# A Conformer block on one core: its depthwise convolution on TensorE in four token phases and plain float32, with more taps on ScalarE and Pool

## The chip, the cores and the metric

The kernel runs on one core of one Trainium2 chip. The metric is the device time of one execution in microseconds (us). The median of three runs before the change is 1697.9 us (1696.76 to 1698.34).

## What is computed

The program is a two-part model on 512 tokens of 1024 channels in float32. The part that the change touches is the first thing that runs, the convolution module:

```
def conformer_conv(h, w_pw1, b_pw1, w_dw, b_dw, ln_g, ln_b, w_pw2, b_pw2):
    u = h @ w_pw1 + b_pw1
    a, gate = jnp.split(u, 2, axis=-1)
    u = a * jax.nn.sigmoid(gate)
    u = lax.conv_general_dilated(
        u, w_dw[:, None, :], window_strides=(1,), padding=[(CONV_WIDTH - 1, 0)],
        dimension_numbers=("NWC", "WIO", "NWC"), feature_group_count=CONV_CHANNELS) + b_dw
    u = jax.nn.silu(layernorm(u, ln_g, ln_b))
    return u @ w_pw2 + b_pw2
```

`h` is the RMS-normed input and `CONV_WIDTH` is 31: each channel is convolved with its own 31 taps over the tokens. After it come a SwiGLU layer, dilated attention, another SwiGLU layer, a retention and pooling mixer and a gated feed-forward layer. They are about nine tenths of the time and the change leaves them alone.

## The kernel before

Channels lie on the 128 partitions and the 512 tokens along them, so the 1024 channels are eight tiles, j = 0 to 7. A large matrix product is made in three passes: each operand is split into a rounded high part and the rest (`whi`, `wlo` of the weights; `xh`, `xl` of the activations), and `mm3` multiplies high by high, high by rest and rest by high. `Stream` brings weights: SP loads a chunk into one of four `raw` buffers, ScalarE writes `whi`, and VectorE (for some chunks Pool) writes `wlo` and so frees the buffer.

In the conv stage the order on TensorE is the list `SEQ`. `g3` is the group of matmuls of tile 3 (an `a` half and a gate half, 48 matmuls into two PSUM banks of a ring of six). `conv_start` then calls `gated`: VectorE multiplies the gate half by the row norm (`tg`), ScalarE takes the sigmoid, VectorE multiplies the `a` half (`ta`, into SBUF), and a last VectorE instruction adds the bias, multiplies the two and writes `up`. The banks of the group come free when VectorE has read them.

From `up` the tiles go two ways:

- Tiles 0, 2, 4 and 5 (`JV`): 31 multiply-adds over shifted views of `up` (`conv_tile`), in two chains `ca` and `cb` in PSUM on VectorE. `POOLT[j]` of the taps are made by ScalarE (the product `tp`) and Pool (the sum `cp`) and added to the rest in `end`. `keep_up` decides by estimated costs how many of these instructions are put in after each half-tick of matmuls.
- Tiles 1, 3, 6 (`JP`) and 7 (`JS`): `to_phases` reorders `up` by SP DMAs so that the partition holds 2 token phases x 64 channels. TensorE multiplies by 128x128 matrices that Pool builds from the taps (`matrices`, buffers `dg`), again in high and low parts (`c1a` and `c1b` in `SEQ` are the two channel groups of tile 1). ScalarE copies the result out of PSUM, SP DMAs reorder it back into `cx`, and one VectorE instruction (`back`) adds the bias and the mean shift `nm0` and writes `cc`.

All DMAs stand in one queue, SP's, in program order, and a DMA that waits holds up all behind it. In it are also six DMAs (`bias_vectors`, `bd` and `be`) that write a table for the later attention through DRAM and read it back. VectorE, ScalarE and Pool each run strictly in program order too. `shift_of_first` makes `nm0` from tile 0 by one matmul (`m`). The layer norm then takes its sums from the squares (`ssq`) and the sum of all tiles (`lnb`, by Pool); its first matmul on all tiles is `lne`.

Of the kernel before, what the change touches and what calls it, by code (L numbers as in the profile page):

```python
# [50 lines left out]
PARTS = 2  # L51
# [6 lines left out]
class Meter:  # L58
# [144 lines left out]
def phases(w):  # L203

    r = np.zeros((2, 64, len(JP) + 1, 2, CW + 1), w.dtype)
    for n, j in enumerate(JP + (JS,)):
        t = w[:, 128 * j:128 * j + 128].reshape(CW, 2, 64).transpose(2, 1, 0)
        r[0, :, n, :, 1:] = t
        r[1, :, n, :, :CW] = t
# [60 lines left out]
def body(nc, tc, A, out):  # L270
# [3 lines left out]
    with ctx:  # L274
# [275 lines left out]
        with tc.tile_pool(name="c1", bufs=1) as c1, tc.tile_pool(name="c1s", bufs=1, side="right") as c1s:  # L550
# [3 lines left out]
            def utile(name, shape=(128, PAD + S), dt=F32):  # L554
                return c1.tile(list(shape), dt, tag="u", name=name, bufs=NU)
# [3 lines left out]
            ct = [c1s.tile([128, S + (PAD if j in JP + (JS,) else 0)], F32, name=f"cc{j}") for j in range(KD)]  # L559
# [41 lines left out]
            def high_part(t):  # L601

                h = utile("hp", t.shape, F32R)
                ACT.activation(out=h, in_=t, func=AF.Copy)
                return h.bitcast(F32)

            V.tensor_tensor(out=wpl, in0=wp, in1=high_part(wp), op=ALU.subtract)

            def matrices(key, n, w, wl, idt):

                d = []
                for src in (w, wl):
                    t = c1.tile([128, 2048], F32R, tag="dg", name="dg", bufs=6)
                    d.append(t)
                    m = idt.shape[1]
                    for a in range(0, n, n // 2 if n % 2 == 0 else n):
                        b = min(n, a + (n // 2 if n % 2 == 0 else n))

                        def build(t=t, src=src, a=a, b=b):
                            G.tensor_tensor(  # L620
                                out=t[:, m * a:m * b].rearrange("p (a b) -> p a b", b=m),
                                in0=idt.unsqueeze(1).to_broadcast([128, b - a, m]),
                                in1=src[:, a:b].unsqueeze(2).to_broadcast([128, b - a, m]),
                                op=ALU.mult,
                            )

                        mat_q.append((key, build))
                dgs[key] = d
# [110 lines left out]
            def gated(j, pa, pg, dst):  # L739
                tg = tmp.tile([128, S], F32, tag="t1", name="tg")  # L740
                V.tensor_tensor(out=tg, in0=pg, in1=R, op=ALU.mult)
                ACT.activation(out=tg, in_=tg, func=AF.Sigmoid, bias=col("b_pw1", 8 + j))
                ta = tmp.tile([128, S], F32, tag="t2", name="ta")
                V.tensor_tensor(out=ta, in0=pa, in1=R, op=ALU.mult)
                run_q(dve_q, 1)
                cut = (lambda v: v) if len(dst.shape) == 2 else (lambda v: v.rearrange("c (s p) -> c p s", p=2))
                V.scalar_tensor_tensor(out=dst, in0=cut(ta), scalar=col("b_pw1", j), in1=cut(tg), op0=ALU.add, op1=ALU.mult)
# [17 lines left out]
            def to_phases(j, a):  # L765

                t = ct[j]
                tv = t.rearrange("p (g s) -> p g s", g=2)
                av = a.rearrange("c (p s) -> c p s", p=2)
                for g in range(2):  # L770
                    for p in range(2):
                        nc.sync.dma_start(out=tv[64 * p:64 * p + 64, g], in_=av[64 * g:64 * g + 64, p])

                def parts():
                    if j == JS:
                        ACT.activation(out=tj[:, :, 0], in_=tv, func=AF.Copy)
                        V.tensor_tensor(out=tj[:, :, 1], in0=tv, in1=tj[:, :, 0].bitcast(F32), op=ALU.subtract)
                        return
                    h, l = utile("uth", dt=F32R), utile("utl", dt=F32R)
                    ACT.activation(out=h, in_=t, func=AF.Copy)  # L780
                    V.tensor_tensor(out=l, in0=t, in1=h.bitcast(F32), op=ALU.subtract)
                    ud[j] = [x.rearrange("p (g s) -> p g s", g=2) for x in (h, l)]

                after(PARTS, parts)

            def conv_phases(j, g):
                if g == 0:
                    bc[j] = xbank("oj")
                o = bc[j].rearrange("p (g s) -> p g s", g=2)[:, g]
                dh, dl = built((j, g))  # L790
                h, l = ud[j]
                for d in range(HP + 1):
                    c = slice(128 * d, 128 * d + 128)
                    mm3(o, dh[:, c], dl[:, c], h[:, g, d:d + HS], l[:, g, d:d + HS], d == 0, d == HP)
                if g == 1:
                    y, x = cc[j], utile("cx", (128, S))
                    ACT.copy(y, bc[j])
                    yv = y.rearrange("p (g s) -> p g s", g=2)
                    xv = x.rearrange("c (q s) -> c q s", q=2)
                    for g in range(2):  # L800
# [29 lines left out]
            units = [(int(x[1]), "ab".index(x[2])) for x in SEQ.split() if x[0] == "c"]  # L830
# [17 lines left out]
            for x in SEQ.split():  # L848
# [16 lines left out]
            def conv_half(h, n0=0, n1=64):  # L865
                ov = o7[h].rearrange("p (g l s) -> p g l s", g=2, l=2)
                for n in range(n0, min(n1, 2 * (HP + 1))):
                    g, d = n // (HP + 1), n % (HP + 1)
                    c = slice(128 * d, 128 * d + 128)
                    s_ = slice(128 * h + d, 128 * h + d + 128)  # L870
                    PE.matmul(ov[:, g], djs[g][0][:, c], tj[:, g, :, s_], start=(d == 0), stop=False)
                    PE.matmul(ov[:, g, 0], djs[g][1][:, c], tj[:, g, 0, s_], start=False, stop=(d == HP))

            def half_out(h):
                ov = o7[h].rearrange("p (g l s) -> p g l s", g=2, l=2)
                y = tmp.tile([128, S], F32, tag="t1", name="y7")
                z = y[:, 256:512].rearrange("p (g s) -> p g s", g=2)
                y = y[:, 0:256].rearrange("p (g s) -> p g s", g=2)
                ACT.copy(z, ov[:, :, 1])
                V.tensor_tensor(out=y, in0=ov[:, :, 0], in1=z, op=ALU.add)  # L880
                y7[h] = y
# [25 lines left out]
            zs = [c1.tile([128, 4, S], F32R, tag="dg", name="zs", bufs=6) for _ in range(4)]  # L907
# [733 lines left out]
```

## Time and profile before

| | before |
|---|---|
| profiled execution | 1698.02 us, its span 1696.2 us |
| TensorE busy | 1655.6 us, 98% of the span |
| VectorE busy | 884.8 us, 52% |
| ScalarE busy | 577.7 us, 34% |
| Pool busy | 187.3 us, 11% |
| granted TensorE clock | 0.989 of full |

Busy time says how long an engine had something in it; it does not say what ended last. The conv stage lies in the first 185 us of the span, and there the shares are others: in the first 180 us TensorE is busy for 160.7 us, VectorE for 149.6 us and Pool for 119.0 us.

### The profile page before, as it was taken

To read this page: it belongs to the slowest core of one execution; us is meant where nothing else is said; L and a number is where in the kernel's file an instruction comes from. 1 tells how busy PE (TensorE), PEld (TensorE's weight loads), DVE (VectorE), ACT (ScalarE), POOL (GpSimd) and SP (SyncE) were. 2 spreads that over 40 slices of the span, in tenths; PEclk is the share of its full clock that TensorE was granted. 3 is DMA by queue.
4 is the path that set the end of the run, shared out by engine and by line. 5 is a ranking of instruction groups with operands and counts; after the bars stand their busy time and mean duration, and the time that the engine had idled before them with its cause. 6 is when DMAs were issued, how large, how long until landed. Compare 5 with 4: busy or idle time off the path is not lost.

```text
span 1696.2 us, 20102 instructions
## 1 busy us (share of the span) xinstructions
PE 1655.6 (98%) x8044; PEld 1391.1 (82%) x8044; DVE 884.8 (52%) x1277; ACT 577.7 (34%) x858; POOL 187.3 (11%) x152
## 2 busy tenths in 40 slices
PE   8988999999999999999999999999999999999997
PEld 6877888888888888888888888888888888888886
DVE  7898654444443445654444443346775545444226
ACT  4133532323322334343323323234543534333210
POOL 4778200000000000000000000000322200000000
PEclk9989999999999999999999999999999999999999
DMA  6322133333232342123333322332232233333321
GB/s 185 113 75 64 39 112 100 99 100 98 86 102 94 93 120 80 51 87 100 100 100 99 100 89 92 106 117 82 63 102 61 83 105 100 100 100 100 99 87 50
DMA packets 154822, 158.11 MB, mean 93 GB/s; under 512 B 6393, under 2 KB 147304, under 8 KB 154728
## 3 DMA queue, kind: packets, MB, share of 16 engines
q1 hardware_dynamic: 154728, 156.83, 30.3%
q8 instruction: 63, 1.03, 0.3%
q14 instruction: 31, 0.25, 0.1%
HBM read 152.79 MB, written 3.95 MB: 92 GB/s over the span
## 4 chain that ended last, share of the span: by engine, by line
PE 81%; DVE 11%; ACT 3%; issue 2%; SPq 1%; DMA 1%; POOL 1%; DVEq 0%; ACTq 0%; POOLq 0%
PE mm L73 69%; PE dn L73 6%; DVE cb L73 2%; PE pv L73 2%; DVE wlo L73 2%; DVE ca L73 2%; PE o L73 1%; PE po L73 1%; DVE cc L73 1%; DVE y L73 1%; ACT whi L120 1%; PE s L73 1%; DVE P L73 1%; DVE up L73 1%; DVE rp L73 0%
## 5 line engine op out<-in xcount | busy, mean ns | idle before, releaser
L73 DVE TENSOR_TENSOR wlo<-raw,whi 128x1024 fp32r<-128x1024 f32 (+1 forms) x278 | 336.0, 1222 | 520.7 <-ACT whi L120 520.1
L73 PE MATMUL mm<-xh,whi 128*128 128x512 f32 (+1 forms) x1472 | 572.4, 389 | 1.8 <-ACT xh L580 1.7
L73 PE MATMUL mm<-xl,whi 128*128 128x512 f32 (+1 forms) x1472 | 568.8, 386 | 2.4 <-POOL xl L73 1.9
L73 PE MATMUL mm<-xh,wlo 128*128 128x512 f32 (+1 forms) x1472 | 568.9, 386 | 1.9 <-DVE wlo L73 1.9
L120 ACT ACTIVATE whi<-raw 128x1024 fp32r<-128x1024 f32 (+1 forms) x282 | 285.8, 1031 | 520.6 <-PE mm L73 324.8
L73 PEld LDWEIGHTS mm<-xl,whi 128*128 128x128 f32 x1472 | 278.4, 189 | 59.4 <-DVE xl L73 3.1
L73 PEld LDWEIGHTS mm<-xh,whi 128*128 128x128 f32 x1472 | 278.7, 189 | 58.4 <-ACT xh L580 2.1
L73 PEld LDWEIGHTS mm<-xh,wlo 128*128 128x128 f32 x1472 | 278.2, 189 | 57.9 <-DVE wlo L73 2.5
L73 PE MATMUL mm<-hh,whi 128*128 128x512 f32 x352 | 136.9, 389 | 0.0
L73 PE MATMUL mm<-hl,whi 128*128 128x512 f32 x352 | 136.9, 389 | 0.0
L73 PE MATMUL mm<-hh,wlo 128*128 128x512 f32 x352 | 136.9, 389 | 0.0
L73 POOL TENSOR_TENSOR r<-v,mhalf 128x4 f32<-128x4 f32 x9 | 13.8, 1531 | 993.2 <-DVE v L73 993.2
L73 PEld LDWEIGHTS mm<-hh,wlo 128*128 128x128 f32 x352 | 66.1, 188 | 13.8
L73 PEld LDWEIGHTS mm<-hl,whi 128*128 128x128 f32 x352 | 66.1, 188 | 13.7
L73 PEld LDWEIGHTS mm<-hh,whi 128*128 128x128 f32 x352 | 66.1, 188 | 13.6
L73 PE MATMUL dn<-whi,gh 128*128 128x512 f32 x176 | 68.7, 390 | 0.9 <-DVE a L73 0.9
L73 PE MATMUL dn<-wlo,gh 128*128 128x512 f32 x176 | 68.6, 390 | 0.1
L73 PE MATMUL dn<-whi,gl 128*128 128x512 f32 x176 | 68.5, 389 | 0.0
L970 ACT ACTIVATE hh<-b 128x512 fp32r<-128x512 f32 x44 | 27.8, 632 | 79.5 <-DVE b L73 79.5
L73 DVE TENSOR_TENSOR b<-mm,R 128x512 f32<-128x512 f32 x44 | 30.2, 685 | 44.5 <-PE mm L73 44.5
L966 ACT ACTIVATE a<-a 128x512 f32<-128x512 f32 x44 | 27.8, 632 | 72.6 <-DVE a L73 72.6
L73 DVE TENSOR_TENSOR hl<-b,hh 128x512 fp32r<-128x512 f32 x44 | 30.5, 692 | 30.8 <-ACT hh L970 30.8
(265 smaller groups left out, 1881.6 us busy)
## 6 DMA issues: line engine op xcount, KB each, us to landing
raw<-in_ffn_w_gate SPq DMA_DIRECT2D x44, 512.0 KB, 4.2
raw<-in_ffn_w_up SPq DMA_DIRECT2D x44, 512.0 KB, 3.8
raw<-in_w_up SPq DMA_DIRECT2D x44, 512.0 KB, 4.0
raw<-in_ffn_w_down SPq DMA_DIRECT2D x40, 512.0 KB, 3.5
raw<-in_w_down SPq DMA_DIRECT2D x22, 512.0 KB, 3.3
raw<-in_w_in SPq DMA_DIRECT2D x20, 512.0 KB, 3.6
raw<-in_attn_w_qkv SPq DMA_DIRECT2D x18, 512.0 KB, 3.8
raw<-in_conv_w_pw SPq DMA_DIRECT2D x30, 256.0 KB, 6.3
```

What stands on the lines that cost most here:

```text
L73: return fn(*args, **kw)
L120: self.nc.scalar.activation(out=hv, in_=raw, func=AF.Copy)
L966: ACT.activation(out=a, in_=a, func=AF.Silu)
L970: ACT.activation(out=hh[j], in_=b, func=AF.Copy)
```

## The change

Tiles 1, 3 and 6 go through TensorE in four token phases x 32 channels instead of two x 64, and in plain float32 with one matmul where there were three with split operands. The matrices of a tile are four groups of nine, 128x128, and are multiplied with 128 tokens each. Tile 7 stays in two phases, but also in plain float32. So the splits of the phase data (`uth`, `utl`, `tj`) and of the taps (`wpl`) go. The reordering of tiles 1, 3 and 6 takes 16 DMAs of 32 partitions each way instead of 4 of 64. The taps on ScalarE and Pool of tiles 0, 2, 4, 5 go from 4, 0, 3, 6 to 7, 8, 8, 8. `gated` writes the product of the `a` half back into its PSUM bank and reads it from there. `SEQ` names the four groups, and the cost estimate counts a plain float32 matmul four times. The line of the helper that records VectorE, Pool and TensorE instructions moves from L73 to L79.

```diff
-SEQ = "g0 g1 g2 g3 c1a c1b g4 g5 c3a g6 c3b g7 c6a c6b"
-POOLT = {0: 4, 1: 2, 3: 4, 5: 6, 4: 3, 2: 0}
+SEQ = "g0 g1 g2 g3 c1ab c1cd g4 g5 c3ab g6 c3cd g7 c6ab c6cd"
+POOLT = {0: 7, 2: 8, 4: 8, 5: 8}
+NPH = 4
+PPAD = 32
+NB = 36
+DPB = 5
...
-            self.us += max(n, 256 if self.fixed == 0 else 0) * self.rate + self.fixed
+            if self.fixed == 0:
+                n = max(4 * n if args[1].dtype == F32 else n, 256)
+            self.us += n * self.rate + self.fixed
...
-                ta = tmp.tile([128, S], F32, tag="t2", name="ta")
-                V.tensor_tensor(out=ta, in0=pa, in1=R, op=ALU.mult)
+                V.tensor_tensor(out=pa, in0=pa, in1=R, op=ALU.mult)
                 run_q(dve_q, 1)
...
-                V.scalar_tensor_tensor(out=dst, in0=cut(ta), scalar=col("b_pw1", j), in1=cut(tg), op0=ALU.add, op1=ALU.mult)
+                V.scalar_tensor_tensor(out=dst, in0=cut(pa), scalar=col("b_pw1", j), in1=cut(tg), op0=ALU.add, op1=ALU.mult)
...
-            def to_phases(j, a):
-
-                t = ct[j]
-                tv = t.rearrange("p (g s) -> p g s", g=2)
-                av = a.rearrange("c (p s) -> c p s", p=2)
-                for g in range(2):
-                    for p in range(2):
-                        nc.sync.dma_start(out=tv[64 * p:64 * p + 64, g], in_=av[64 * g:64 * g + 64, p])
-
-                def parts():
...
-                    h, l = utile("uth", dt=F32R), utile("utl", dt=F32R)
-                    ACT.activation(out=h, in_=t, func=AF.Copy)
-                    V.tensor_tensor(out=l, in0=t, in1=h.bitcast(F32), op=ALU.subtract)
...
+            def to_phases(j, a, n):
+
+                m = 128 // n
+                tv = (tj if j == JS else ct[j]).rearrange("p (g s) -> p g s", g=n)
+                av = a.rearrange("c (p s) -> c p s", p=n)
+                for g in range(n):
+                    for p in range(n):
+                        nc.sync.dma_start(out=tv[m * p:m * p + m, g], in_=av[m * g:m * g + m, p])
+                ud[j] = tv
...
-                for d in range(HP + 1):
-                    c = slice(128 * d, 128 * d + 128)
-                    mm3(o, dh[:, c], dl[:, c], h[:, g, d:d + HS], l[:, g, d:d + HS], d == 0, d == HP)
-                if g == 1:
+                for d in range(steps):
+                    PE.matmul(o, d4[:, 128 * d:128 * d + 128], ud[j][:, g, d:d + n], start=(d == 0), stop=(d == steps - 1))
+                if g == NPH - 1:
...
-                    for g in range(2):
-                        for q in range(2):
-                            nc.sync.dma_start(out=xv[64 * g:64 * g + 64, 1 - q], in_=yv[64 * q:64 * q + 64, g])
+                    for g in range(NPH):
+                        for q in range(NPH):
+                            nc.sync.dma_start(out=xv[32 * g:32 * g + 32, NPH - 1 - q], in_=yv[32 * q:32 * q + 32, g])
```

**SP's queue, from the bias table to tile 7, before.** `raw` are weight chunks, `cc<-up` is `to_phases` (`cc_159` is tile 3, `cc_162` tile 6, `cc_163` tile 7) and `cx<-cc` the way back (`cc_157` is tile 1).

```order
L757 DMA bd_514<-bv 4x256
L759 DMA be_516<-bd_514 512x1x256
L103 DMA raw<-in_conv_w_pw 128x4x128 x4
L772 DMA cc_159<-up_627 64x271 x4
L802 DMA cx<-cc_157 64x256 x4
L103 DMA raw<-in_conv_w_pw 128x4x128 x4
L103 DMA raw<-in_conv_w_pw 128x4x256 x4
L772 DMA cc_162<-up_1104 64x271 x4
L802 DMA cx<-cc_159 64x256 x4
L103 DMA raw<-in_conv_w_pw 128x4x256 x2
L772 DMA cc_163<-up_1272 64x271 x4
L802 DMA cx<-cc_162 64x256 x4
```

The same stretch of SP's queue in the changed kernel:

```order
L762 DMA bd_530<-bv 4x256
L764 DMA be_532<-bd_530 512x1x256
L109 DMA raw<-in_conv_w_pw 128x4x128 x4
L777 DMA cc_159<-up_673 32x136 x16
L796 DMA cx<-cc_157 32x128 x16
L109 DMA raw<-in_conv_w_pw 128x4x128 x4
L109 DMA raw<-in_conv_w_pw 128x4x256 x4
L777 DMA cc_162<-up_1088 32x136 x16
L796 DMA cx<-cc_159 32x128 x16
L109 DMA raw<-in_conv_w_pw 128x4x256 x2
L777 DMA tj<-up_1238 64x271 x4
L796 DMA cx<-cc_162 32x128 x16
```

The order of the blocks is the same; each block of four for tiles 1, 3 and 6 is now one of sixteen.

**VectorE's queue around the return of tile 1, before.** `up_948` is tile 5, `ca` and `cb` over `up_846` are taps of tile 4, and `cc_157<-cx` is `back` of tile 1.

```order
L73 SCALAR_TENSOR_TENSOR up_948<-ta,cv,tg 128x512
L73 SCALAR_TENSOR_TENSOR ca<-up_846,cv,ca 128x512
L73 SCALAR_TENSOR_TENSOR cb<-up_846,cv,cb 128x512
L73 SCALAR_TENSOR_TENSOR ca<-up_846,cv,ca 128x512
L73 TENSOR_TENSOR cc_156<-cc_156,nm_164 128x512
L73 SCALAR_TENSOR_TENSOR cb<-up_846,cv,cb 128x512
L73 SCALAR_TENSOR_TENSOR ca<-up_846,cv,ca 128x512
L73 SCALAR_TENSOR_TENSOR cb<-up_846,cv,cb 128x512
L73 SCALAR_TENSOR_TENSOR cc_157<-cx,cv,nm_164 128x2x256
```

VectorE's queue around the same `back` in the changed kernel; `cc_158` is tile 2 and `up_848` tile 4:

```order
L79 SCALAR_TENSOR_TENSOR cc_158<-up_561,cv,ca 128x512
L79 TENSOR_TENSOR cc_158<-cc_158,cb 128x512
L79 TENSOR_TENSOR cc_158<-cc_158,cp_569 128x512
L79 TENSOR_TENSOR cc_158<-cc_158,nm_164 128x512
L79 SCALAR_TENSOR_TENSOR cc_157<-cx,cv,nm_164 128x4x128
L79 MEMSET up_848 128x30
L79 TENSOR_TENSOR tg<-mm,R 128x512
L79 TENSOR_TENSOR mm<-mm,R 128x512
L79 SCALAR_TENSOR_TENSOR up_848<-mm,cv,tg 128x512
```

`back` of tile 1 stood behind the gating of tile 5 and now stands ahead of the gating of tile 4, because `nm0` is made earlier (its matmul `m` moves from behind `c3b` into `g3`).

**VectorE's queue around the gating of tile 7 in the changed kernel.** `up_1238` is tile 7, `up_956` tile 5, and `cc_159<-cx` is `back` of tile 3. Before, `back` of tile 3 also stood a few rows ahead of tile 7's gating.

```order
L79 SCALAR_TENSOR_TENSOR ca<-up_956,cv,ca 128x512
L79 SCALAR_TENSOR_TENSOR cc_159<-cx,cv,nm_164 128x4x128
L79 SCALAR_TENSOR_TENSOR cb<-up_956,cv,cb 128x512
L79 SCALAR_TENSOR_TENSOR ca<-up_956,cv,ca 128x512
L79 SCALAR_TENSOR_TENSOR cb<-up_956,cv,cb 128x512
L79 MEMSET up_1238 128x2x15
L79 TENSOR_TENSOR tg<-mm,R 128x512
L79 TENSOR_TENSOR mm<-mm,R 128x512
L79 SCALAR_TENSOR_TENSOR ca<-up_956,cv,ca 128x512
L79 SCALAR_TENSOR_TENSOR up_1238<-mm,cv,tg 128x2x256
```

What moved between the two: `back` of tile 3 now has only four taps and the gating between itself and `up` of tile 7.

## Rows read from the trace of the kernel before

**Rows 1.** Windows: stretch, length, busy us and count by engine, clock, DMA share, GB/s.

```profile
100.00:110.00 10.00, 3.89 (x7) 2.48 (x8) 10.00 (x15) 4.45 (x7) 9.50 (x7) 0.57 0.33 107
150.00:160.00 10.00, 4.71 (x24) 4.75 (x25) 9.97 (x14) 3.47 (x6) 9.76 (x7) 0.66 0.29 80
```

**Rows 2.** Waits, 0 to 185 us: waiter, releaser, total us, times, longest.

```profile
ACT uth L780 <- DMA cc<-up: 18.3, 3, 11.8
```

**Rows 3.** Timeline of SP's queue, 28 to 175 us: start, us, DMA, count.

```profile
44.58 2.44 SPq L772 DMA_DIRECT2D cc<-up  x4
...
49.46 0.35 SPq L757 DMA_DIRECT2D bd<-bv  x1
...
71.68 5.79 SPq L103 DMA_DIRECT2D raw<-in_conv_w_pw  x4
77.52 3.16 SPq L772 DMA_DIRECT2D cc<-up  x4
```

**Rows 4.** Timeline of SP's queue, single DMAs, three narrow stretches.

```profile
18.05 0.33 SPq L595 DMA_DIRECT2D rb<-in_rel_bias  x1
18.48 0.40 SPq L103 DMA_DIRECT2D raw<-in_conv_w_pw  x1
...
146.52 0.59 SPq L772 DMA_DIRECT2D cc<-up  x1
147.16 0.59 SPq L772 DMA_DIRECT2D cc<-up  x1
...
597.62 3.94 SPq L997 DMA_DIRECT2D b<-be  x8
```

**Rows 5.** DMA issues by line, 0 to 185 us: count, KB each, median us to landing.

```profile
cc<-up SPq DMA_DIRECT2D x16, 67.8 KB, 2.1
...
cx<-cc SPq DMA_DIRECT2D x12, 64.0 KB, 2.8
```

**Rows 6.** Timeline of VectorE, 24 to 185 us: start, us, instruction.

```profile
42.60 1.95 DVE L73 SCALAR_TENSOR_TENSOR up<-ta,cv,tg 128x512 f32<-128x512 f32 x1
...
56.02 0.67 DVE L73 TENSOR_TENSOR ta<-mm,R 128x512 f32<-128x512 f32 x1
56.62 0.74 DVE L73 SCALAR_TENSOR_TENSOR ca<-up,cv,ca 128x512 f32<-128x512 f32 x1
57.27 0.74 DVE L73 SCALAR_TENSOR_TENSOR up<-ta,cv,tg 128x512 f32<-128x512 f32 x1
...
139.69 0.74 DVE L73 SCALAR_TENSOR_TENSOR cc<-cx,cv,nm 128x512 f32<-128x512 f32 x1
```

**Rows 7.** Groups of instructions by form, 0 to 185 us: busy us, mean ns.

```profile
L73 POOL TENSOR_TENSOR dg<-delta,wpl 128x1024 fp32r<-128x1024 f32 x16 | 33.1, 2087 | 0.0
...
L73 DVE TENSOR_TENSOR wlo<-raw,whi 128x1024 fp32r<-128x1024 f32 x14 | 21.7, 1564 | 0.6 <-ACT whi L120 0.6
...
L73 POOL TENSOR_TENSOR cp<-cp,tp 128x512 f32<-128x512 f32 x10 | 14.5, 1449 | 4.5 <-ACT tp L684 4.1
L73 DVE SCALAR_TENSOR_TENSOR up<-ta,cv,tg 128x512 f32<-128x512 f32 x8 | 10.8, 1351 | 0.2 <-ACT tg L742 0.2
...
L73 DVE TENSOR_TENSOR utl<-cc,uth 128x542 fp32r<-128x542 f32 x3 | 2.9, 965 | 8.0 <-ACT uth L780 8.0
```

**Rows 8.** Chain that ended last, 0 to 185 us: start, us, what.

```profile
155.28 10.64 PE o L73 x74
...
169.17 0.84 PE lne L73 x8
...
172.80 0.96 PE lnq L73 x8
```

**Rows 9.** Timeline of TensorE, two stretches.

```profile
71.85 0.40 PE L73 MATMUL mm<-xh,whi 128*128 128x512 f32 x1
...
97.67 0.28 PE L73 MATMUL oj<-utl,dg 128*128 128x256 f32 x1
...
98.03 0.28 PE L73 MATMUL oj<-utl,dg 128*128 128x256 f32 x1
```

More of the change, by code (lines that the diff above doesn't have):

```diff
@@ L203, in phases, with four_phases @@
 def phases(w):
[L205 to L209, printed above, removed]
+    r = np.zeros((2, 64, 2, CW + 1), w.dtype)
+    t = w[:, 128 * JS:128 * JS + 128].reshape(CW, 2, 64).transpose(2, 1, 0)
+    r[0, :, :, 1:] = t
+    r[1, :, :, :CW] = t
+    return r.reshape(128, -1)
+def four_phases(w):
+    r = np.zeros((NPH, 32, len(JP), 4, NB), w.dtype)
+    for n, j in enumerate(JP):
+        t = w[:, 128 * j:128 * j + 128].reshape(CW, 4, 32).transpose(2, 1, 0)
+        for p in range(NPH):
+            r[p, :, n, :, 5 - p:5 - p + CW] = t
     return r.reshape(128, -1)
@@ L558, in body @@
             V.memset(rb[32:33, :], NEG)
-            ct = [c1s.tile([128, S + (PAD if j in JP + (JS,) else 0)], F32, name=f"cc{j}") for j in range(KD)]
+            ct = [c1s.tile([128, S + (PPAD if j in JP else 0)], F32, name=f"cc{j}") for j in range(KD)]
             cc = [t[:, 0:S] for t in ct]
@@ L572, in wcol @@
                 return col("w_dw", KD * t + j)
+            nc.sync.dma_start(out=wq, in_=A["c_phase4"])
             nc.sync.dma_start(out=wp, in_=A["c_phase"])
             G.tensor_tensor(out=delta, in0=ident[:, 0:64], in1=ident[:, 64:128], op=ALU.add)
+            G.tensor_tensor(out=delta4, in0=delta[:, 0:32], in1=delta[:, 32:64], op=ALU.add)
             st.wait = WAIT
@@ L599, in body, with matrices, build @@
             dve_q, pool_q, mat_q, up, ud, dgs, bc = [], [], [], {}, {}, {}, {}
-            def high_part(t):
-                h = utile("hp", t.shape, F32R)
-                ACT.activation(out=h, in_=t, func=AF.Copy)
[L605 to L628, printed above, removed]
+            def matrices(key, w, idt, tag, bufs, parts):
+                n, m = w.shape[1], idt.shape[1]
+                t = c1.tile([128, 2048 if tag == "dg" else NB * 32], F32, tag=tag, name=tag, bufs=bufs)
+                for a in range(0, n, n // parts):
+                    b = a + n // parts
+                    def build(a=a, b=b):
+                        G.tensor_tensor(
+                            out=t[:, m * a:m * b].rearrange("p (a b) -> p a b", b=m),
+                            in0=idt.unsqueeze(1).to_broadcast([128, b - a, m]),
+                            in1=w[:, a:b].unsqueeze(2).to_broadcast([128, b - a, m]),
+                            op=ALU.mult,
+                        )
+                    mat_q.append((key, build))
+                dgs[key] = t
             def conv_tile(j, taps, acc, name, t, init, last=None):
@@ L829, in body @@
             after(BIAS, bias_vectors)
-            units = [(int(x[1]), "ab".index(x[2])) for x in SEQ.split() if x[0] == "c"]
+            units = [(int(x[1]), "abcd".index(g)) for x in SEQ.split() if x[0] == "c" for g in x[2:]]
             units += [(JS, 0), (JS, 1)]
@@ L836, in next_unit @@
                     j, g = units.pop(0)
-                    o = NW * (JP + (JS,)).index(j) + g * (CW + 1)
-                    matrices((j, g), CW + 1, wp[:, o:o + CW + 1], wpl[:, o:o + CW + 1], delta)
-            for _ in range(3):
+                    if j == JS:
+                        matrices((j, g), wp[:, (CW + 1) * g:(CW + 1) * (g + 1)], delta, "dg", 5, 2)
+                    else:
+                        o = NB * (4 * JP.index(j) + g)
+                        matrices((j, g), wq[:, o:o + NB], delta4, "dp", DPB, 1)
+            for _ in range(DPB - 1):
                 next_unit()
@@ L856, in body @@
                 else:
-                    conv_phases(j, "ab".index(x[2]))
-                    next_unit()
+                    for g in x[2:]:
+                        conv_phases(j, "abcd".index(g))
+                        next_unit()
                     tick()
@@ L865, in conv_half @@
             def conv_half(h, n0=0, n1=64):
-                ov = o7[h].rearrange("p (g l s) -> p g l s", g=2, l=2)
+                ov = o7[h][:, 0:256].rearrange("p (g s) -> p g s", g=2)
                 for n in range(n0, min(n1, 2 * (HP + 1))):
                     g, d = n // (HP + 1), n % (HP + 1)
-                    c = slice(128 * d, 128 * d + 128)
                     s_ = slice(128 * h + d, 128 * h + d + 128)
-                    PE.matmul(ov[:, g], djs[g][0][:, c], tj[:, g, :, s_], start=(d == 0), stop=False)
-                    PE.matmul(ov[:, g, 0], djs[g][1][:, c], tj[:, g, 0, s_], start=False, stop=(d == HP))
+                    PE.matmul(ov[:, g], djs[g][:, 128 * d:128 * d + 128], ud[JS][:, g, s_], start=(d == 0), stop=(d == HP))
             def half_out(h):
[L875 to L881, printed above, removed]
+                y = tmp.tile([128, S], F32, tag="t1", name="y7")[:, 0:256]
+                ACT.copy(y, o7[h][:, 0:256])
+                y7[h] = y.rearrange("p (g s) -> p g s", g=2)
             def half_swap(h):
@@ L906, in body @@
             half_out(0)
-            zs = [c1.tile([128, 4, S], F32R, tag="dg", name="zs", bufs=6) for _ in range(4)]
+            zs = [c1.tile([128, 4, S], F32R, tag="dg", name="zs", bufs=5) for _ in range(4)]
             zh = [zs[2 * (k // 4)][:, k % 4] for k in range(KD)]
```

47 lines of the change are left out of this document (21 added, 26 removed).

## The prediction

> **What bounds the kernel now.** I read the page first, then windows of 10 us over the conv stage. Outside that stage TensorE is busy without a break and nothing changes, so only the stage can give or take time. In it TensorE stands still twice: between 100 and 110 us it is busy 3.89 of 10 us and between 150 and 160 us 4.71 of 10, while VectorE is busy for the whole of both stretches [rows 1]. The granted clock there is 0.57 and 0.66 of full, so each pause costs something beyond itself. VectorE sets the end in this stage, not TensorE.
>
> The waits say what VectorE itself hangs on. ScalarE's copies of the phase data waited 18.3 us in three waits for the reordering DMAs [rows 2]. SP's timeline shows why: the six DMAs of the bias table hold the queue from 49.46 to 71.68 us, four weight DMAs follow, and only at 77.52 us do the four of tile 3 start; the four that bring tile 1 back stand behind them [rows 3]. So the reader is to see two limits: VectorE's work, and SP's one queue, whose blocks come late.
>
> **What the change takes off VectorE.** 18 taps leave it (13 before, 31 now on ScalarE and Pool). A tap takes its place for 0.65 us, the distance of two starts [rows 6]: 11.7 us. Three splits `utl` go, 2.9 us [rows 7]. The multiply that writes `up` averages 1.351 us over eight [rows 7], but 0.74 us where nothing disturbs it and 1.95 us at 42.60 [rows 6]; with one operand in PSUM it has the form of a tap, so I price it at 0.66: eight times 0.7, about 5.5 us. One add of `cp` comes in for tile 2 (about 0.7). Together VectorE loses about 19 us of work. The product into PSUM (`mm<-mm,R`) I leave at the 0.6 us of `ta` [rows 6]; were it a quarter dearer, that would be 1.2 us over eight.
>
> **TensorE.** Three matmuls of 256 columns with split operands take 0.36 us [rows 9], so the 96 of one tile take 11.5 us. A plain float32 matmul of 128 columns shows as two instructions; the four of `lnq` take 0.96 us [rows 8], 0.24 each. 36 of them make 8.6 us a tile, about 9 us less over three tiles; were each twice as dear, 17 us more. Tile 7's first half has 32 for 7.7 us where 74 of the old instructions took 10.64 [rows 8]. None of this is in the sum: TensorE has idle time to hide either, as long as VectorE or SP comes later.
>
> **Pool.** It drops 32 builds of 2.09 us and makes four of that size and twelve that are an eighth larger (about 36 us in place of 67), and its adds go from 10 to 27 at 1.45 us (39 in place of 14.5) [rows 7]. That is 6 us less; I take nothing.
>
> **What the change puts on SP's queue.** Six blocks of four DMAs become six of sixteen. What one DMA costs SP is the number on which all hangs; call it s. Between tensors in SBUF the starts lie 0.64 us apart (146.52 to 147.16), for 64 partitions of about 1 KB [rows 4]. No DMA there has 32 partitions and a quarter of the bytes. The dearest row is thus 0.64. The cheapest is the small `rb` (32 partitions of 48 bytes from DRAM), 0.43 us from its start to the next [rows 4]; eight DMAs of `b<-be`, 128 partitions of 512 bytes, take 3.94 us, 0.49 each [rows 4]. The new ones have the rows of the last and the SBUF-to-SBUF form of the first, so I take 0.55. A block of sixteen then holds the queue for 8.8 us where four took 2.44 to 3.16 [rows 3].
>
> One rule of the Trainium skill stands against this price. DMA: Bandwidth & Descriptors, section Issuing engines are not separate DMA queues, says that the time a sequencer takes to start a DMA is usually small beside the DMA itself. Here a start takes 0.59 us and landing 2.1 [rows 4, 5], and sixteen starts outlast one landing. By the rule a block would cost little more than its landing, and the sum would be near that of the first rival below, 1678 us; by the rows it is the one that follows.
>
> **The walk.** `up` of tile 1 starts at 42.60 [rows 6] and ends near 43.3. SP: sixteen DMAs to 52.1; four weight DMAs (2.4, from the end of the block at 44.58 to 49.46) to 54.5; the bias table (22.2) to 76.7; four weights (5.8) to 82.5 [rows 3]; sixteen for tile 3 to 91.3; sixteen for the return of tile 1 to 100.1; landed 2.8 us later [rows 5], at 102.9. In VectorE's new order `back` of tile 1 stands ahead of the gating of tile 4, and VectorE gets to it about when tile 4's matmuls are done: near 83 us, an estimate from their start at 71.85 and 48 matmuls of 512 columns at twice the 0.12 us of those of 256 [rows 9]. VectorE's queue stands for some 20 us. Behind it wait the gating of tile 4, so the banks for `g6`, so TensorE.
>
> VectorE goes on: `back` 0.74, then `tg`, product, wait for the sigmoid and `up` 2.1, to 105.7. From there to `up` of tile 6 the order has 30 taps (19.5), three `wlo` at 1.56 (4.7), two adds (1.4) and two gatings of 1.9 (3.8): 29.4 us, 135.1. SP then sends tile 6 and brings tile 3 back: 17.6 us, and 2.8 to land, 155.5. VectorE has only about 10 us of work before `back` of tile 3, so it stands again, about 10 us. Behind that are four taps, `tg`, product, `up` of tile 7: with `back` 5.2 us, 160.7. Tile 7's DMAs are unchanged: two starts and a landing, 3.4 us. TensorE starts tile 7 at 164.1, where it started at 155.28 [rows 8].
>
> From there to `lne` it took 13.9 us (155.28 to 169.17, rows 8), which gives 178.0. The other road to `lne` is tile 6's return: behind tile 7's four DMAs (160.7 + 2.6) sixteen more, 8.8, landing 2.8, `back` 0.74, a square (like a tap) 0.66 and two Pool adds 2.9: 179.2. The later one counts: 179.2 against 169.17 is 10.0 us later. After `lne` nothing differs but some matmuls of tile 7, so the delay goes to the end. The profiled execution is 1698.02 us, its span 1696.2, and the median 1697.9, so the sum is 1698 + 10 = **1708 us**. The same walk with s = 0.43 has six blocks less 1.9 us each and gives 1697; with 0.64, 1717. Equal time lies near s = 0.45.
>
> **Rivals.**
>
> Faster, 1678 us: the DMAs are not late. If a start cost SP in proportion to bytes, a quarter of 0.64, a block of sixteen would take 2.6 us as now. Tile 1's return would land near 84, when VectorE comes to it; tile 6's `up` follows at 117, tile 3's return lands at 125 ahead of VectorE, tile 7 starts near 135 and `lne` comes near 149, 20 us earlier: the 19 us of VectorE's work would all be gained. It decides once s is below about 0.2. For it: the matching total of bytes. Against it: `rb` with 1.5 KB still takes 0.33 us to start [rows 4]. In between, with s of 0.2 to 0.43, lie gains of 1 to 20 us.
>
> The same, 1697 us: SP pays 0.43 to 0.48, the price of the small DMA, and what VectorE saves is spent on standing at two `back`s.
>
> Slower by Pool, about 1704 us: the 27 adds each need a tap from ScalarE, and VectorE stands at `cc<-cc,cp`. Pool's list in the stage, 39 us of adds, 36 of builds, about 10 of `wlo` and 18 of sums for the norm, makes 103 us of the some 130 until `lne`, so only an add of twice 1.45 us would make it the last, with a cost of some 6 us beyond what VectorE's wait hides.
>
> **How the numbers follow.** Chances: the forecast (SP's blocks, s above 0.46) 0.66; Pool in place of it 0.04; the same 0.13; faster 0.17, most of it in between the two prices. About 0.2% (3.4 us) is what a measurement can tell from no change. So slower 0.70, same 0.13, faster 0.17. The forecast's own range is 1701 to 1719; the whole range is 1691 to 1718, which leaves out the gains of more than 7 us and the dearest end.
>
> **What would show it.** Right: blocks of sixteen `cc<-up` and `cx<-cc` of 7 to 10 us on SP; VectorE idle for 10 us or more ahead of `cc<-cx` of tile 1 and again ahead of that of tile 3, released by a DMA; TensorE idle ahead of `g6` with VectorE as releaser; tile 7 starting after 155 us; `up` at 0.7 us. Wrong: starts of 0.3 us or less, or `cc<-cx` finding its data landed; then VectorE is busy to the end and the gain is that of the first rival.

## The result and the profile after

The changed kernel takes 1717.78 us (median, 1716.01 to 1719.22) where the kernel before took 1697.33 in the same session: a ratio of 1.0124, 95% interval 1.0108 to 1.0140, slower by 20.4 us. The sign and the range held; the size did not, the forecast was 10 us. Its profiled execution took 1718.52 us, with a span of 1715.5.

SP's queue in the changed kernel (start, us, DMA, count), to set against [rows 3]:

```profile
44.19 10.09 SPq L777 DMA_DIRECT2D cc<-up  x16
...
84.62 11.00 SPq L777 DMA_DIRECT2D cc<-up  x16
95.72 10.03 SPq L796 DMA_DIRECT2D cx<-cc  x16
...
144.42 10.95 SPq L777 DMA_DIRECT2D cc<-up  x16
155.47 10.02 SPq L796 DMA_DIRECT2D cx<-cc  x16
...
174.92 10.43 SPq L796 DMA_DIRECT2D cx<-cc  x16
```

Six blocks hold the queue for 62.5 us. Divided by 96 starts that is 0.65 us for one, the price of the dearest row known ahead (0.64, [rows 4]), although each now moves 16 or 17 KB in place of 64 or 68 [rows 5]:

```profile
cc<-up SPq DMA_DIRECT2D x48, 17.0 KB
...
cx<-cc SPq DMA_DIRECT2D x48, 16.0 KB
```

VectorE's timeline: the three returns (`cc<-cx`) and the `up` of tiles 4, 6 and 7, with the idle time ahead in brackets; compare [rows 6]:

```profile
107.03 1.13 DVE L79 SCALAR_TENSOR_TENSOR cc<-cx,cv,nm 128x512 f32<-128x512 f32 x1 [23.57 <-DMA cx<-cc]
...
109.55 0.75 DVE L79 SCALAR_TENSOR_TENSOR up<-mm,cv,tg 128x512 f32<-128x512 f32 x1 [0.18 <-ACT tg L748]
...
143.19 1.14 DVE L79 SCALAR_TENSOR_TENSOR up<-mm,cv,tg 128x512 f32<-128x512 f32 x1
...
166.72 1.14 DVE L79 SCALAR_TENSOR_TENSOR cc<-cx,cv,nm 128x512 f32<-128x512 f32 x1 [12.54 <-DMA cx<-cc]
...
171.60 0.75 DVE L79 SCALAR_TENSOR_TENSOR up<-mm,cv,tg 128x512 f32<-128x512 f32 x1
...
186.79 1.12 DVE L79 SCALAR_TENSOR_TENSOR cc<-cx,cv,nm 128x512 f32<-128x512 f32 x1 [11.38 <-DMA cx<-cc]
```

VectorE stands 47.5 us in front of three DMAs. What that does to TensorE is seen in windows of 10 us (columns as in [rows 1]), in the start of tile 7 and in the chain's `lne`:

```profile
90.00:100.00 10.00, 8.40 (x56) 7.47 (x54) 0.00 (x0) 0.00 (x0) 1.56 (x1) 1.00 0.12 27
100.00:110.00 10.00, 1.09 (x3) 0.83 (x3) 2.79 (x5) 1.73 (x3) 0.96 (x1) 0.69 0.38 102
160.00:170.00 10.00, 0.00 (x0) 0.00 (x0) 3.29 (x6) 0.63 (x1) 1.34 (x2) 0.59 0.37 119
```

```profile
175.12 3.11 PE L79 MATMUL o<-tj,dg 128*128 128x128 f32 x13 [16.21 <-DMA tj<-up]
```

```profile
193.85 0.79 PE lne L79 x8
```

VectorE does nothing at all from 90 to 100 us; TensorE runs out of work behind it (1.09 us of 100 to 110, nothing of 160 to 170). Before, both stretches around 100 and 150 showed the opposite, a full VectorE and a waiting TensorE. Tile 7 starts at 175.12 (155.28 before, [rows 8]) and `lne` comes at 193.85 (169.17).

The groups by form (busy us, mean ns | idle ahead) show that the work itself became cheaper:

```profile
L79 POOL TENSOR_TENSOR cp<-cp,tp 128x512 f32<-128x512 f32 x27 | 39.2, 1451 | 5.7 <-ACT tp L690 4.1
L79 POOL TENSOR_TENSOR dp<-delta,wq 128x1152 f32<-128x1152 f32 x12 | 26.2, 2217 | 0.0
...
L79 DVE SCALAR_TENSOR_TENSOR up<-mm,cv,tg 128x512 f32<-128x512 f32 x8 | 7.2, 896 | 0.4 <-ACT tg L748 0.4
L79 DVE TENSOR_TENSOR mm<-mm,R 128x512 f32<-128x512 f32 x8 | 5.5, 687 | 0.0
```

The waits of the same stretch (waiter, releaser, total, times, longest):

```profile
ACT sq L505 <- DVE cc L79: 52.9, 6, 21.6
POOL ssq L79 <- ACT sq L505: 50.9, 5, 17.5
DVE cc L79 <- DMA cx<-cc: 47.5, 3, 23.6
...
PEld o L79 <- POOL dg L79: 16.4, 1, 16.4
PE o L79 <- DMA tj<-up: 16.2, 1, 16.2
```

ScalarE's squares (`sq`) wait for VectorE's `cc`, and Pool's sums of squares (`ssq`) wait for them: both queues stand behind the same returns. One wait was not foreseen: in the standstill ahead of tile 7, TensorE's weight load also waited 16.4 us for Pool's matrices of that tile. They stand in Pool's queue behind `ssq` of tile 3. Pool was not busy, it was queued behind the same late DMA. This wait did not set the end by itself: Pool began the matrices at 171.1, three of them took 6.1 us, and tile 7's data came only at 175.1.

### The profile page after: what moved, and what is told of

The parts are those of the page before. It is cut to its first block, busy times and chain, and to the rows that moved or that the text cites. A ratio compares the mean times of both kernels' runs of the same rounds, so it can differ in the third digit from the quotient of the medians.

```text
span 1715.5 us, 20055 instructions
## 1 busy us (share of the span) xinstructions
PE 1648.0 (96%) x7972; PEld 1381.5 (81%) x7972; DVE 863.2 (50%) x1251; ACT 586.7 (34%) x871; POOL 181.7 (11%) x154
## 4 chain that ended last, share of the span: by engine, by line
PE 80%; DVE 9%; SPq 4%; ACT 3%; issue 2%; DMA 1%; POOL 1%; DVEq 0%; ACTq 0%; POOLq 0%
PE mm L79 69%; PE dn L79 6%; SPq L777 2%; PE pv L79 2%; SPq L796 2%; DVE wlo L79 1%; DVE cb L79 1%; DVE ca L79 1%; PE po L79 1%; ACT whi L126 1%; DVE y L79 1%; PE s L79 1%; DVE cc L79 1%; SPq L109 1%; DVE P L79 1%
## 5 line engine op out<-in xcount | busy, mean ns | idle before, releaser
L79 DVE TENSOR_TENSOR wlo<-raw,whi 128x1024 fp32r<-128x1024 f32 (+1 forms) x278 | 334.8, 1218 | 525.4 <-ACT whi L126 525.3
L79 PE MATMUL mm<-xh,whi 128*128 128x512 f32 (+1 forms) x1472 | 574.7, 390 | 19.2 <-ACT sq L505 10.5
L79 PE MATMUL mm<-xl,whi 128*128 128x512 f32 (+1 forms) x1472 | 571.3, 388 | 2.6 <-POOL xl L79 1.9
L79 PE MATMUL mm<-xh,wlo 128*128 128x512 f32 (+1 forms) x1472 | 570.7, 388 | 0.5 <-DVE wlo L79 0.5
L79 PEld LDWEIGHTS mm<-xh,whi 128*128 128x128 f32 x1472 | 280.1, 190 | 76.5 <-issue 18.2
L79 PEld LDWEIGHTS mm<-xl,whi 128*128 128x128 f32 x1472 | 280.0, 190 | 59.2 <-DVE xl L79 2.8
L79 PEld LDWEIGHTS mm<-xh,wlo 128*128 128x128 f32 x1472 | 279.8, 190 | 57.3 <-DVE wlo L79 1.1
L79 PE MATMUL mm<-hh,whi 128*128 128x512 f32 x352 | 136.9, 389 | 0.0
L79 PE MATMUL mm<-hl,whi 128*128 128x512 f32 x352 | 136.9, 389 | 0.0
L79 PE MATMUL mm<-hh,wlo 128*128 128x512 f32 x352 | 136.9, 389 | 0.0
L79 POOL TENSOR_TENSOR r<-v,mhalf 128x4 f32<-128x4 f32 x9 | 13.8, 1531 | 993.4 <-DVE v L79 993.4
L79 PEld LDWEIGHTS mm<-hl,whi 128*128 128x128 f32 x352 | 66.1, 188 | 13.8
L79 PEld LDWEIGHTS mm<-hh,wlo 128*128 128x128 f32 x352 | 66.1, 188 | 13.7
L79 PEld LDWEIGHTS mm<-hh,whi 128*128 128x128 f32 x352 | 66.1, 188 | 13.6
L79 PE MATMUL dn<-whi,gh 128*128 128x512 f32 x176 | 68.7, 390 | 0.9 <-DVE a L79 0.9
L79 PE MATMUL dn<-wlo,gh 128*128 128x512 f32 x176 | 68.6, 390 | 0.1
L79 PE MATMUL dn<-whi,gl 128*128 128x512 f32 x176 | 68.5, 389 | 0.0
L79 DVE TENSOR_TENSOR b<-mm,R 128x512 f32<-128x512 f32 x44 | 30.2, 686 | 44.2 <-PE mm L79 44.2
L79 DVE TENSOR_TENSOR hl<-b,hh 128x512 fp32r<-128x512 f32 x44 | 30.5, 692 | 30.8 <-ACT hh L964 30.8
```

## The experiments

The theory to test: SP pays about 0.65 us for each start whatever its bytes, so the returns land late, and VectorE, TensorE and Pool stand in their queues behind them. Against it: the plain float32 matmuls, Pool's adds or the product in PSUM make the time; or the DMAs cost by bytes. Each ratio is to the kernel before, timed on the same chip beside it. Differences to the changed kernel are between medians taken beside different runs of the kernel before, whose medians lie 2.4 us apart (1695.9 to 1698.3).

**1. The change in two phases.** Everything else of the change stays; the matrices and the DMAs' slices follow the number of phases.

```diff
-NPH = 4
-PPAD = 32
-NB = 36
+NPH = 2
+PPAD = 30
+NB = 32
...
-                            nc.sync.dma_start(out=xv[32 * g:32 * g + 32, NPH - 1 - q], in_=yv[32 * q:32 * q + 32, g])
+                            nc.sync.dma_start(out=xv[64 * g:64 * g + 64, NPH - 1 - q], in_=yv[64 * q:64 * q + 64, g])
```

> The changed kernel with tiles 1, 3 and 6 in two token phases again (six blocks of four DMAs of 64 partitions in place of six of sixteen), everything else of the change kept: plain float32, the new taps, the gating in PSUM. Theory (SP pays 0.64 us for each of sixteen starts, and VectorE stands at the returns): blocks of 2.5 us, the stands of 23.6, 12.5 and 11.4 us ahead of the three returns are gone or below 4 us each, and VectorE's 19 us less work are gained, so 1675 to 1688 us, although a plain float32 tile costs TensorE 32 x 0.5 = 16 us in place of 9. Rival (plain float32, Pool's adds or the gating in PSUM make the time): 1710 us or more.

Measured: 1691.61 us, ratio 0.9962 (0.9947 to 0.9977): 26 us under the changed kernel, faster than before, 3.6 us above the expected range. The blocks are back at 2.4 to 3.3 us and VectorE meets the returns of tiles 1 and 3 without a wait (it waits 15.8 us for that of tile 6, whose matmuls end late). What holds it now is seen in the windows and in a row of the chain:

```profile
110.00:140.00 30.00, 29.70 (x123) 24.74 (x124) 27.38 (x39) 12.43 (x17) 26.18 (x16) 0.92 0.18 51
140.00:170.00 30.00, 30.00 (x206) 27.76 (x205) 6.40 (x14) 4.54 (x7) 7.13 (x6) 1.00 0.20 57
```

```profile
141.41 13.82 PE oj L79 x64
```

TensorE is full from 110 to 170 us: a two-phase tile of plain float32 takes 13.8 us. So a part of VectorE's gain was not to be had with this form.

**2. The other half: old phases, new taps and the product in PSUM.**

```diff
-POOLT = {0: 4, 1: 2, 3: 4, 5: 6, 4: 3, 2: 0}
+POOLT = {0: 7, 2: 8, 4: 8, 5: 8}
...
-                V.tensor_tensor(out=ta, in0=pa, in1=R, op=ALU.mult)
+                V.tensor_tensor(out=pa, in0=pa, in1=R, op=ALU.mult)
...
```

> The kernel before with two edits of the change only: the new taps on ScalarE and Pool and the gating in PSUM; its two phases and split operands stay. Theory: blocks of four on SP, VectorE loses 11.7 + 5.5 us, the time is 1680 to 1690 us, if Pool carries 27 adds (39 us) beside its 32 builds (67 us); if it does not, up to 1697. Rival (taps or gating cost the time): 1705 us or more.

Measured: 1719.98 us, ratio 1.0127 (1.0110 to 1.0144). The theory's range was missed by 23 us and more: here the rival holds. The waits and the window say why:

```profile
DVE cc L73 <- POOL cp L73: 19.7, 2, 15.9
```

```profile
140.00:170.00 30.00, 21.21 (x166) 20.88 (x164) 6.66 (x8) 12.89 (x20) 28.40 (x21) 0.90 0.13 36
```

Pool is busy 28.4 of 30 us while VectorE does 6.7: with 32 builds of split matrices (65 us) and 27 adds (37 us) Pool is the bound in this stretch, and VectorE stands 19.7 us at `cc<-cc,cp`. In this program the taps pay only together with the change to plain float32, which halves the builds: in the changed kernel the builds take 26 us for the three tiles and some 8 for tile 7.

**3. The product in PSUM alone**, on the kernel before (the second edit of the diff above).

> The kernel before with the gating product left in PSUM, alone. Theory: up takes 0.75 to 0.9 us in place of 1.35, some 4 to 5 us less work of VectorE, which is the bound before: 1691 to 1696 us. Rival (the product into PSUM is dearer, or banks come free later): 1698 to 1703. Beside the run with new taps as well (1720.0), this one tells what the taps do on the old two phases: by it they cost the difference.

Measured: 1692.00 us, ratio 0.9965 (0.9952 to 0.9978), 5.9 us faster. One `up` of the kernel before (tile 3, at 67.17 us), and the group of `up` in this kernel:

```profile
67.17 2.17 DVE L73 SCALAR_TENSOR_TENSOR up<-ta,cv,tg 128x512 f32<-128x512 f32 x1
```

```profile
L73 DVE SCALAR_TENSOR_TENSOR up<-mm,cv,tg 128x512 f32<-128x512 f32 x8 | 5.9, 742 | 0.2 <-ACT tg L742 0.2
```

Eight times 1351 less 742 ns [rows 7] are 4.9 us. So the product in PSUM is a gain, and the taps on the old phases cost the difference to experiment 2, 28 us.

**4. Twice the DMAs, half the bytes each.**

```diff
-                        nc.sync.dma_start(out=tv[m * p:m * p + m, g], in_=av[m * g:m * g + m, p])
...
+                        for c in (slice(0, 68), slice(68, 136)):
+                            nc.sync.dma_start(out=tv[m * p:m * p + m, g, c], in_=av[m * g:m * g + m, p, c])
```

The returns are cut in the same way; tile 7 is left as it was.

> The changed kernel with each of the 96 DMAs of tiles 1, 3 and 6 cut into two halves of its columns: six blocks of 32 DMAs with half the bytes each, the same data in the same places. Theory (SP pays about 0.64 us for each start, whatever the bytes): a block holds the queue for 20.5 us; back of tile 1 some 30 us later than in the changed kernel (107.0), back of tile 3 some 50, back of tile 6 some 60; 1770 to 1785 us. Rival (cost by bytes): blocks of 10 us as before, 1715 to 1722 us. Rival (starts of less than 1 KB a row are cheaper, 0.43 as the small one of the table): blocks of 13.8 us, 1735 to 1742.

Measured: 1779.77 us (the median of two runs, 1777.16 and 1782.38), ratio 1.0481 (1.0456 to 1.0505). SP's queue and the first return on VectorE:

```profile
43.81 20.86 SPq L782 DMA_DIRECT2D cc<-up  x32
...
116.52 20.16 SPq L802 DMA_DIRECT2D cx<-cc  x32
```

```profile
137.92 1.12 DVE L80 SCALAR_TENSOR_TENSOR cc<-cx,cv,nm 128x512 f32<-128x512 f32 x1 [45.86 <-DMA cx<-cc]
```

These are 0.65 and 0.63 us a start with some 8 KB each. Cost by bytes is out; so is a cheaper price for short rows. `back` of tile 1 is 30.9 us later for three blocks that are each some 10 us longer.

**5. The returns started by ScalarE.**

```diff
-                            nc.sync.dma_start(out=xv[32 * g:32 * g + 32, NPH - 1 - q], in_=yv[32 * q:32 * q + 32, g])
+                            nc.scalar.dma_start(out=xv[32 * g:32 * g + 32, NPH - 1 - q], in_=yv[32 * q:32 * q + 32, g])
```

> The changed kernel with the 48 DMAs that bring tiles 1, 3 and 6 back started by ScalarE in place of SP. Theory: SP has three blocks of 10 us fewer, tile 1's return no longer stands behind tile 3's block and lands before VectorE comes to it, tile 6's up comes some 20 us earlier; ScalarE pays some 10 us for each block, which delays sigmoids and taps. 1685 to 1703 us. Rival (the matmuls, Pool or the gating make the time): 1715 to 1722; rival (ScalarE is hit as hard as SP was): 1710 to 1718.

Measured: 1710.63 us, ratio 1.0077 (1.0061 to 1.0094), above the expected range and at the lower end of the rival that ScalarE is hit as hard. ScalarE's queue:

```profile
70.92 11.12 ACTq L796 DMA_DIRECT2D cx<-cc  x16
82.08 1.06 ACT L126 ACTIVATE whi<-raw 128x1024 fp32r<-128x1024 f32 x1 [11.20 <-DMA cx<-cc]
```

Sixteen starts take ScalarE 11.1 us (0.70 each), in which it computes nothing; the sigmoid of tile 4 comes late and VectorE waits 8.0 us for it ahead of `up`. `back` of tile 1 came at 89.2 in place of 107.0, but the price moved with the starts.

**6. `back` planned later.** SP's queue keeps its order; VectorE meets the returns of tiles 1 and 3 further back.

```diff
-BACK = 2.5
+BACK = 7
```

> The changed kernel with back planned 7 steps behind its tile's last matmuls in place of 2.5: VectorE meets the return of tile 1 behind the gating of tiles 4 and 5, that of tile 3 behind the gating of tile 7. SP's queue is the same, DMA by DMA. Theory (the blocks are late, but most of the price comes from VectorE's queue that stands behind a late return): the stand of 23.6 us ahead of back of tile 1 goes, tile 6's up comes about 20 us earlier (near 123 in place of 143), the time falls to 1690 to 1702. Rival (the length of SP's queue alone sets the end, whatever VectorE does): 1713 to 1720.

Measured: 1705.09 us, ratio 1.0050 (1.0032 to 1.0068): 12.7 us of the loss went with the place of `back` in VectorE's queue, which had stood behind a late return. The rest stays; the time is 3 us above the expected range. VectorE's `up` of tile 6, and the waits:

```profile
138.39 1.13 DVE L79 SCALAR_TENSOR_TENSOR up<-mm,cv,tg 128x512 f32<-128x512 f32 x1
```

```profile
DVE wlo L79 <- ACT whi L126: 19.8, 6, 12.7
...
ACT whi L126 <- DMA raw<-in_conv_w_pw: 16.3, 5, 10.3
```

It comes 5 us earlier, not 20: with `back` out of the way the weights' DMAs are the late ones. They stand behind the same two blocks on SP, which end at 105.9.

**7. The bias table's DMAs grouped**, three writes and then three reads, in the changed kernel and in the kernel before:

```diff
+                firsts = []
...
                     nc.sync.dma_start(out=d1, in_=t)
+                    firsts.append((L, d1))
+                for g, (L, d1) in enumerate(firsts):
                     d2 = tc.dram_tile([4, 128, L], F32, name=f"be{g}")
```

> The changed kernel with the six DMAs of the bias table in the order three writes, three reads back, so that SP waits for one landing in place of three; nothing else is moved. Theory (tile 3's block and tile 1's return are late on SP's queue, and VectorE stands for that): the table holds SP for 8 to 10 us in place of 22.8, tile 3's block starts some 13 us earlier, the stand of 23.6 us ahead of back of tile 1 falls to some 10, 1704 to 1710 us. Rival (the matmuls, Pool or the gating make the time): 1716 to 1720.

> The kernel before with the same reordering of the bias table's DMAs. Theory: tile 3's block of four starts when its data is there, near 68 in place of 77.5, the 8 us that VectorE stood at the split of tile 3 are gone, of which VectorE, busy for most of the stage, gains 3 to 8 us: 1689 to 1695 us. Rival (VectorE's work alone sets the end of the stage): 1696 to 1699.

Measured: 1712.42 us, ratio 1.0085 (1.0070 to 1.0100), on the changed kernel, and 1691.33 us, ratio 0.9963 (0.9949 to 0.9977), on the kernel before. SP in the changed kernel with grouping:

```profile
55.97 1.15 SPq L763 DMA_DIRECT2D bd<-bv  x3
59.89 10.21 SPq L767 DMA_DIRECT2D be<-bd  x3
70.63 8.90 SPq L109 DMA_DIRECT2D raw<-in_conv_w_pw  x4
79.58 10.65 SPq L780 DMA_DIRECT2D cc<-up  x16
```

```profile
SPq L109 <- DVE ca L79: 4.9, 1, 4.9
```

The three reads take 10.2 us by themselves, and the table still holds SP for 14.1 us where 8 to 10 were expected. The four weight DMAs behind it then wait 4.9 us for VectorE (before it frees a `raw` buffer), and take 8.9 us in place of 5.1. So tile 3's block starts 5.0 us earlier (79.58 for 84.62) and not 13; `back` of tile 1 comes 5.4 us earlier (101.63), and the time falls by 5.4. From SP's queue to the end the step is about one to one, within what the intervals can tell; the size of the expected gain was wrong. On the kernel before, the wait of VectorE at `utl` of tile 3 falls from 8.0 [rows 7] to 2.4 us, and the end comes 6.6 us earlier: SP was a second limit there.

```profile
79.99 0.72 DVE L73 TENSOR_TENSOR utl<-cc,uth 128x542 fp32r<-128x542 f32 x1 [2.38 <-ACT uth L783]
```

**8. The returns on TensorE.** Sixteen matmuls with columns of the identity take the place of sixteen DMAs; `back` reads the bank.

```diff
-                            nc.sync.dma_start(out=xv[32 * g:32 * g + 32, NPH - 1 - q], in_=yv[32 * q:32 * q + 32, g])
...
+                                PE.matmul(px4[0][32 * g:32 * g + 32, NPH - 1 - q], ident[:, 32 * q:32 * q + 32], yv[:, g], start=True, stop=True)
```

> The changed kernel with tiles 1, 3 and 6 brought back by TensorE: sixteen plain float32 matmuls of 32 x 128 with columns of the identity into a bank, which back reads, in place of sixteen DMAs. Four phases, plain float32, taps and gating stay; SP keeps three blocks of sixteen. Theory: the three stands of VectorE at the returns (23.6, 12.5, 11.4 us) go, TensorE pays some 16 x 0.22 = 3.5 us more a tile; the end comes 25 to 35 us earlier, 1682 to 1694 us. Rival (the four phases' matmuls, Pool or the gating make the time): 1712 or more.

> The same with the bias table's DMAs grouped as three writes and three reads, so that tile 3's block starts some 5 us earlier. If TensorE still waits for that block, up to 5 us less than with the return on TensorE alone (1677 to 1690 us); if TensorE or VectorE is the bound by then, the same time.

Measured: 1690.96 us, ratio 0.9972 (0.9960 to 0.9984), and with the grouped table 1689.23 us, ratio 0.9957 (0.9943 to 0.9972). The return of tile 1 on VectorE, and the matmuls of tile 1's four phases, in the first of the two:

```profile
80.83 1.13 DVE L79 SCALAR_TENSOR_TENSOR cc<-x,cv,nm 128x512 f32<-128x512 f32 x1
```

```profile
63.18 8.20 PE L79 MATMUL oj<-cc,dp 128*128 128x128 f32 x72
```

No idle time ahead of `back`, at 80.83 in place of 107.03. The four phases, plain float32, the new taps and the product in PSUM are all still in, and the kernel is faster than before: taking three of the six blocks off SP gives 27 us. The grouped table adds less than the intervals can tell.

**9. Versions that might beat both.** The kernel before with its two cheap gains, and the two-phase form with the grouped table:

```diff
-                V.tensor_tensor(out=ta, in0=pa, in1=R, op=ALU.mult)
+                V.tensor_tensor(out=pa, in0=pa, in1=R, op=ALU.mult)
...
+                    firsts.append((L, d1))
+                for g, (L, d1) in enumerate(firsts):
```

> The kernel before with the gating product in PSUM and the bias table grouped, the two edits that gave 5.9 and 6.6 us alone. If both come off VectorE's time in the stage they add up: 1684 to 1687 us. If one is hidden behind the other: 1690 to 1692.

> The changed kernel in two phases of plain float32 with the bias table grouped. In the two-phase run TensorE was busy for nearly the whole stage except 6 us between 80 and 110; by that only these 6 us can be gained: 1686 to 1691 us. If the late DMAs of tile 3 still set the end, 5 us or more: 1684 to 1687.

Measured: 1687.59 us, ratio 0.9949 (0.9934 to 0.9964), and 1690.20 us, ratio 0.9964 (0.9952 to 0.9975). The first lies between its two cases, 0.51% against the sum of 0.72%. VectorE's row at `utl` of tile 3 shows where the rest went:

```profile
79.45 0.72 DVE L73 TENSOR_TENSOR utl<-cc,uth 128x542 fp32r<-128x542 f32 x1 [6.12 <-ACT uth L782]
```

With the shorter gating VectorE comes there earlier and waits 6.1 us again, for data that SP brings. In the second, tile 3's block started 4.6 us earlier (71.84 for 76.44) and the time stayed within the intervals, so TensorE's 6 idle us between 80 and 110 in experiment 1 were not SP's; the profile puts them down to VectorE in both (6.46 and 6.45 us). The first has the lowest median; whether it beats the returns on TensorE with the grouped table the intervals don't decide.

## Why the prediction was right in sign and wrong in size

**What bounded the kernel before** was read rightly: VectorE's work and SP's late blocks. Less gating work alone gave 5.9 us, an earlier block alone 6.6.

**SP's price was the step that failed.** The walk took s = 0.55, between a row of the same form with more bytes (0.64) and rows from DRAM with few bytes or other widths (0.43, 0.49). Measured: 62.5 us in 96 starts, 0.65, and 0.63 to 0.66 in blocks of 32 with half the bytes. The row of the same form was the price; the middle had no row of its own. By the prediction's own walk, 0.64 gave 1717; the kernel took 1717.8. That the two agree so well is partly luck: with 0.64 the walk has `lne` 18.7 us later than before, measured it was 24.7, and 5.4 of these were lost again on the way to the end.

The rule of the Trainium skill that was weighed there (DMA: Bandwidth & Descriptors, section Issuing engines are not separate DMA queues: the time to start a DMA is usually small beside the DMA itself) does not describe a block of sixteen: the sixteen starts of tile 1's return took 10.0 us and its last data was used 1.3 us after the block's end. By it the time would have been near 1678.

**The walk, point by point.** `back` of tile 1: forecast 102.9 (landing), measured 107.0, with three blocks of 10 to 11 us ahead in place of 8.8. From `up` of tile 4 to that of tile 6: forecast 29.4 us of work, measured 33.6 (109.55 to 143.19). This second, smaller miss priced rows as undisturbed that were not, and 2.2 us of it are waits of VectorE's `wlo` for ScalarE's `whi`; its parts were not tested one by one. Tile 3's `back`: 155.5 against 166.7. Tile 7's start: 164.1 against 175.1. `lne`: 179.2 against 193.85. Of these last 14.7 us, the six blocks account for 9.7 (62.5 less 52.8) and VectorE's stretch for 4.2. Smaller misses on both sides make up the rest: VectorE had the data of a return 1.2 to 1.4 us after its block ended, where the walk allowed 2.8 three times, and from `back` of tile 6 to `lne` it took 7.1 us in place of 4.3. Of the signs named ahead, the stands at the returns and tile 7's start came as said. The blocks were 10.0 to 11.0 us and not 7 to 10. TensorE stood 10.5 us ahead of `g6`, but the profile names ScalarE's square of tile 1, which itself follows `back`, as what released it.

**From `lne` to the end.** The forecast carried the delay over unchanged. Measured, 24.7 us at `lne` became 19.3 in the span. From the second half of tile 7 (`cc<-p`, at 201.49 and 178.28) to the end, the changed kernel took 1514.0 us and the kernel before 1517.9; the twelve experiments took 1513 to 1517 there. The traces place the loss late: at the matmuls `pr` of a later layer (to 1129.1 and 1152.9) the delay is still 23.8 us, and at the last `lnq` it is 19.5:

```profile
L73 PE MATMUL lnq<-ident,lr x16: 270/348/582, 1307.1 to 1326.7; 128*128 128x128 f32 x16
```

```profile
L79 PE MATMUL lnq<-ident,lr x16: 270/275/398, 1327.8 to 1346.2; 128*128 128x128 f32 x16
```

Why it varies was not tested; the change doesn't touch that part. TensorE is not quite without a break there, as the prediction had it: before, it is busy for 195.4 of the 200 us from 1100 to 1300.

**VectorE's saving** was there and could not be used: it stood 47.5 us instead. `up` was forecast at 0.66 and averaged 0.896, since the writes in four phases take 1.14 where plain ones take 0.75; the gain on eight is 3.6 us, not 5.5.

**TensorE and Pool.** The 36 matmuls of a tile take 8.2 us (forecast 8.6), and leaving them out of the sum was right: the same matmuls are in the 1691.0 us of experiment 8. Pool took 39.2 us of adds, as forecast, and 34.2 of builds (26.2 and, for tile 7, 8.0; forecast about 36), and was not the bound. Experiment 2 shows how near that rival was: with the old builds the same taps put the kernel at 1720.

**How much was VectorE's queue.** Planning `back` later returned 12.7 of the 20 us; what held the rest in that run were the weights behind the blocks, which no run took away alone. Removing three blocks returned 27. So the cause is shown in both directions: more starts, 62 us slower; fewer, 27 us faster. The bytes and the arithmetic are unchanged in the first; in the second TensorE has 48 more matmuls.

## What to carry to other kernels

A finer layout that cuts matmul time multiplies the DMAs that make it: count the starts per queue, price each by the row of the same kind whatever its bytes, and see what else stands in that queue and in the queue of the engine that takes the data. Work that moves to another engine can be paid for by an edit that looks unrelated: here the taps fit on Pool only because plain float32 halved its builds. And where an unknown price lies between two rows, the row with the same endpoints was the one to take here, not the middle.

## What was not expected of the hardware

- A DMA from SBUF to SBUF cost SP nearly the same to start with 8, 16 to 17 or 68 KB: 0.63 to 0.66 and 0.63 to 0.69 us as the mean of a block, and 0.64 between two undisturbed starts [rows 4]. Started by ScalarE it cost 0.63 to 0.74 (10.1 to 11.8 us for sixteen), and ScalarE computed nothing meanwhile.
- The write of `up` with both operands in SBUF took 0.74 to 2.17 us ([rows 6, 7], and the row in experiment 3); with one in PSUM all eight took 0.74 to 0.75 us in experiment 3.
- A plain float32 matmul took 0.23 us for 128 columns (8.20 for 36) and 0.43 for 256 (13.82 for 32), where three of 256 columns with split operands took 0.36 [rows 9].
